# A mixer's queries, pooled input and gates as products of halves, with token-major gated branches

## The chip, the cores and the metric

The kernel runs on one core of a Trainium2 chip. The metric is the device time of one execution in microseconds. A core has five engines that run their own queues of instructions in order: TensorE (PE in the profile, with its weight loads as PEld), VectorE (DVE), ScalarE (ACT), GpSimd (POOL, which here only issues transfers) and SyncE (SP, which issues transfers). Matmuls write PSUM, and VectorE and ScalarE read it from there.

## The reference

A decoder trunk of two layers on 512 tokens of 1024 channels, all float32. Each layer is FFN, mixer, FFN; the FFN is SwiGLU with 2816 hidden channels. The mixer is what changes:

```python
h = rmsnorm(x, ln_mix[l])
z = h @ w_in[l]                       # 1024 -> 512 + 512 + 256 + 2 * 1024
u_pool, q, k, v, gate_logits = jnp.split(z, splits, axis=-1)
a = pool_mixer(u_pool, pool_w[l], pool_scale[l]) @ w_pool_branch[l]
...                                   # q, k: norm per head, rotation of 16 channels
b = swa_sink_attention(q, k, v, sinks[l]) @ w_attn_branch[l]
g_pool, g_attn = jnp.split(jax.nn.sigmoid(gate_logits), N_BRANCHES, axis=-1)
x = x + (g_pool * a + g_attn * b) @ w_out[l]
```

The pooling takes trailing means over 2, 4, 8 and 16 positions in four groups of 128 channels, less the token, then a 128x128 map per group. The attention has 8 query heads of 64 channels on 2 key heads, blocks of 128 tokens that read their own block and the one before, and a sink in the softmax.

## The kernel before

**Precision.** A float32 product is made of three matmuls of a faster float32 form: each operand is split into a high part (a cast on ScalarE, `wh` for weights) and the rest (a subtraction on VectorE, `wl`), and high x high, high x low and low x high are added in PSUM (`term`).

**Products of halves.** `strassen` forms a product whose tokens, inner channels and outer channels are each cut in halves by seven products of sums of halves where eight would be plain. The seven have the names a11, s1, s2, a12, s3, s4, a22 (`ORDER`). Each is 24 matmuls of 512 columns, 12 for each of two weight chunks; the activation is the stationary operand, the weight columns move through, and so the result has tokens on the partitions. After each a step evacuates or combines PSUM. All FFN products and w_out go that way before the change. The mixer's other products are plain: the queries and keys with moving weights, the pooled input (`u`), the gates and the branches with the weights stationary, so that channels are on the partitions (`gemm`, `tile_of`).

**Weights.** `Weights` holds a plan of chunks of 128x1024 (0.5 MB). `prep`, called after each chunk, makes the low part for two chunks ahead (3 buffers), the high part for three ahead (4 buffers), adds the sums of s2 and s4 on VectorE (`add_up`), and lets SP fetch, up to seven chunks in flight. For s1 and s3, POOL issues a second, accumulating transfer onto the chunk, which waits until the first has landed.

**The mixer** (`mix`). After the norm's operands (`Norm.feed`: x is transposed by TensorE, scaled, split), the order is two tiles of `u` begun, keys and values, the rest of `u`, queries, two more tiles of `u`, 16 gate tiles, eight steps of the two branches, then w_out by `strassen`. The row scale of the norm is spread over the partitions by two matmuls (`spread`) and multiplied in at the evacuation of each channel-major tile. Beside the tiles runs side work in generators, and tables of numbers (`HEADS`, `ATT`, `POOL`) say at which half tile each next step of a generator is written into the queues (`side`): normalising the heads, the eight attention steps (`attend`: scores, mask and maximum, exponentials, scaling, transposes of the probabilities, product with the values, split) and the four windows of the pooling. One unit of these tables is 12 matmuls. The instructions keep the order in which the program writes them, engine by engine.

All instructions go through a wrapper, so the profile has one line for them: L97. They are told apart by the names of their tiles: `wh`, `wl` weights; `raw` a loaded chunk; `sums` a sum of halves; `mm` and `sc` PSUM banks of the products; `pt`, `pt_tp`, `pt_pv` PSUM banks for transposes and side work; `xgh`, `xgl`, `more` the norm's operands; `ze`, `zo` gates and branches; `s`, `p`, `den` the attention's.

Of the kernel before, what the change touches and what calls it, by code (L numbers as in the profile page):

```python
# [10 lines left out]
F32 = mybir.dt.float32  # L11
# [17 lines left out]
PLACE = {B11: 0, T1: 1, B21: 2, B22: 3}  # L29
# [17 lines left out]
KEYS = (-3,)  # L47
NORMS = (-1, -1, 1)
HEADS = ((0, 2, 2), (0, 3, 3), (5, 8, 8), (12, 15, 15))
ATT = tuple(tuple(4 + 3 * n + d for d in (0, 1, 2, 5, 6, 9, 10)) for n in range(8))  # L50
POOL = ((-3, -2, 0, 0), (-2, -1, 8, 8), (12, 14, 17, 17), (18, 20, 25, 25))
# [4 lines left out]
C_UT = C_LT + P  # L56
C_COS = C_UT + P
# [5 lines left out]
def _consts():  # L63
# [5 lines left out]
    c[:, C_UT:C_UT + P] = i[:, None] > i[None, :]  # L69
# [50 lines left out]
def trunk(ctx, tc, x0, xT, consts, vecs, rows, w_g4, w_g3, w_d8, w_d6, w_qkv, w_u, w_pool, w_gate, w_br, w_out, out):  # L120
# [14 lines left out]
    onesr = cp.tile([P, P], F32R, name="onesr")  # L135
# [3 lines left out]
    nc.vector.tensor_copy(out=onesr, in_=ones)  # L139
# [44 lines left out]
    class Weights:  # L184
# [3 lines left out]
        def __init__(self):  # L188
# [3 lines left out]
            for l in range(L):  # L192
                for f in range(2):
                    if f == 1:
                        for kind, src, n in (("u", w_u[l], 2), ("qkv", w_qkv[l], 6), ("u", w_u[l, 2:], 2),
                                             ("gate", w_gate[l], 2 * KT), ("br", w_br[l], KT)):
                            for i in range(n):
                                self.add(kind, CH, src[i])
                        self.block(lambda h, k, c, w=w_out[l]: w[h, 2 * k + c], (CH, CH), ORDER)
# [26 lines left out]
        def block(self, w, sizes, order, start=False):  # L226

            name, first = {}, len(self.loads)
            src = {"a11": ((0, 0), None), "s1": ((1, 0), (1, 1)), "s3": ((0, 0), (1, 0)), "a12": ((0, 1), None),
                   "a22": ((1, 1), None), "s2": (None, None), "s4": (None, None)}  # L230
            for k in order:
                for c in range(2):
                    s, m = (None if p is None else w(*p, c) for p in src[k])
                    name[k, c] = self.add(k, sizes[c], s, m)
            for c in range(2):
                name["s2", c]["of"] = name["a11", c], name["s1", c]
                name["s4", c]["of"] = name["s2", c], name["a12", c]
                for k in ("a11", "s1", "a12"):
                    name[k, c]["uses"] += 1
            loads = ("a11", "s1") if start else ("s1", "a11")  # L240
            self.loads[first:] = [name[k, c] for k in (*loads, "a12", "s3", "a22") for c in range(2)]
# [48 lines left out]
        def low(self, upto):  # L290
            while len(self.lo) < min(upto, len(self.hi)):
# [7 lines left out]
                tick(2)  # L299

# [63 lines left out]
    def rsqrt(y, v):  # L364
        for step in rsqrt_steps(y, v):
            step()


    parts = [xp.tile([P, 2, NB], F32, name=f"part{i}") for i in range(2)]

    class Norm:
        def __init__(self, gain, halves):
            self.gain, self.halves = gain, halves
            self.acc = None
            self.h = self.rstd = None
# [3 lines left out]
        def opened(self):  # L379
            if self.h is None:  # L380
                self.h, self.l = (xl.tile([P, KT * S], F32R, name=n) for n in ("xgh", "xgl"))
                form, shape = ("p (i k t) -> p i k t", dict(i=4, k=4)) if self.halves else (
                    "p (q i k t) -> p q i k t", dict(q=4, i=2, k=2))
                self.h, self.l = (t.rearrange(form, **shape) for t in (self.h, self.l))
# [10 lines left out]
        def both(self, i, j):  # L395
            if i in PLACE:
                return [t[:, PLACE[i], 2 * j:2 * j + 2, :].rearrange("p k t -> p (k t)") for t in (self.h, self.l)]
# [6 lines left out]
        def feed(self, q, i, pt):  # L404
# [15 lines left out]
            if not self.halves:  # L420
                halve(*(t[:, q, i].rearrange("p k t -> p (k t)") for t in (self.h, self.l)), scaled(temp("xg")))
                return
# [6 lines left out]
            else:  # L429
                self.keep[3 - i, j] = scaled(temp("xg"))  # L430
                halve(*self.both(B22 if i else B21, j), self.keep[3 - i, j])

# [50 lines left out]
        def split_plain(self, k, b12, src):  # L483
# [5 lines left out]
            else:  # L489
                split(*(t[:, 2:4, k - 4, :] for t in (self.h, self.l)), halves(src), scale=g)  # L490
# [15 lines left out]
        def sums(self, acc=None, pt=None):  # L506
# [11 lines left out]
            if self.halves:  # L518
                self.nrstd = xp.tile([P, NB], F32, name="nrstd")
                slow.extend(rsqrt_steps(self.rstd, v))  # L520
                slow.append(lambda: nc.vector.tensor_scalar(
                    out=self.nrstd, in0=self.rstd, scalar1=-1.0, scalar2=None, op0=ALU.mult
                ))
                return
            rsqrt(self.rstd, v)
            hi, lo = sp.tile([P, NB], F32R, name="rs_h"), sp.tile([P, NB], F32, name="rs_l")
            nc.vector.tensor_copy(out=hi, in_=self.rstd)
            nc.vector.tensor_tensor(out=lo, in0=self.rstd, in1=hi.bitcast(F32), op=ALU.subtract)
            self.diag = [tp.tile([P, NB, P], F32R, name="diag", tag="t") for _ in range(2)]
            for d, r in zip(self.diag, (hi.bitcast(F32), lo)):  # L530
                nc.vector.tensor_tensor(out=d, in0=bc(ident, NB), in1=bc(r, P, 2), op=ALU.mult)

        def spread(self, pr):
            for i, d in enumerate(self.diag):
                nc.tensor.matmul(pr, onesr, d.rearrange("p b t -> p (b t)"), start=i == 0, stop=i == 1)
            self.R = xp.tile([P, S], F32, name="R")
            nc.scalar.copy(out=self.R, in_=pr)

        def terms(self, w):
            return pairs(w, [[t[:, k // 2, :, k % 2, :] for t in (self.h, self.l)] for k in range(KT)])  # L540

# [9 lines left out]
    def left(nm):  # L551
        last = [(lambda bank, q=q: nm.feed(q, 0, bank)) for q in (2, 3)]
        if nm.halves:
            step = lambda f: [(lambda bank, j=j: f(j)) for j in range(2)]
            last = step(nm.t3) + step(nm.t2) + last + step(nm.t3_split) + step(nm.t4)
        pend.extend(last)

    def feeds(nm, *banks):
# [5 lines left out]
        if nm.halves:  # L564
# [3 lines left out]
    def strassen(roles, order, n, sizes, operand, steps, mid={}):  # L568
        A, C, Dd = roles
        bank = {"a11": A, "s2": A, "s3": A, "a22": A, "s1": C, "s4": C, "a12": Dd}  # L570
        seen = set()
        for kind in order:
            pt, first = bank[kind], id(bank[kind]) not in seen
            seen.add(id(pt))
# [25 lines left out]
        order_.reverse()  # L600

    @with_exitstack
    def ffn(ctx, nm, nxt, last):
# [9 lines left out]
        def open_sums():  # L613
            W.sums = sums
            W.low(W.used + LO)
            W.add_up(W.used + HI + 1)
            W.high(W.used + HI)
            W.low(W.used + LO)
            W.load()

        wide = lambda name: ep.tile([P, 2, S], F32, name=name)
        f, ops, turns = {}, {}, []

        rs = lambda b: nm.rstd[:, b:b + 1]
        nrs = lambda b: nm.nrstd[:, b:b + 1]
        count = [0]

        def block(n, i, order, mid):
# [4 lines left out]
            def a11(pt):  # L633
                nc.scalar.copy(out=r, in_=pt)
                if W.sums is None:
                    open_sums()
                return flush
# [47 lines left out]
            turns.append((r, i, 0, n))  # L685
            turned(tile_["p"], i, 1, n)

        def high(name, src, n):

            ops[name] = op.tile([P, 2, 2, S], F32R, name="op", tag=f"op{AT[name]}")  # L690
            hi, lo = (ops[name][:, i, :, :n] for i in range(2))
            nc.scalar.copy(out=hi, in_=src)
            ops[name, "low"] = lambda: nc.vector.tensor_tensor(
                out=lo, in0=src, in1=hi.bitcast(F32), op=ALU.subtract
            )

        def low(name):
            ops.pop((name, "low"))()

        def turned(src, i, t, n):  # L700


            jn = n // P
            for q in range(2):
                for j in range(jn):
                    nc.tensor.transpose(turn[:, q, j * P:(j + 1) * P], src[:, q, j * P:(j + 1) * P], ident)
            pt = turn[:, :, :n]
            if i == 0 and t == 1:
                f["b"] = fp.tile([P, 2, S], F32, name="fb")[:, :, :n]
                nc.scalar.copy(out=f["b"], in_=pt)  # L710
            elif i == 0:
                high("a11", pt, n)
                f["a"] = fp.tile([P, 2, S], F32, name="fa")[:, :, :n]
                nc.vector.tensor_tensor(out=f["a"], in0=pt, in1=f["b"], op=ALU.subtract)
                high("s1", f["a"], n)
            elif t == 1:
                f["c"] = fp.tile([P, 2, S], F32, name="fc")[:, :, :n]
                nc.scalar.copy(out=f["c"], in_=pt)
                nc.vector.scalar_tensor_tensor(
                    out=f["a"], in0=f["a"], scalar=-1.0, in1=f["c"], op0=ALU.mult, op1=ALU.subtract  # L720
                )
                high("s2", f["a"], n)
            else:
                high("a12", pt, n)
                ops["t4"] = lambda: nc.vector.scalar_tensor_tensor(
                    out=f["a"], in0=f["a"], scalar=-1.0, in1=pt, op0=ALU.mult, op1=ALU.subtract
                )

        def flush():
            if turns:  # L730
                turned(*turns.pop(0))

        def plain(n, xt, acc, later):
# [67 lines left out]
            for h, name in ((1, "p"), (0, "r0")):  # L801
# [6 lines left out]
                turns.append((u, 0, h, n))  # L808

        def down(n, final):  # L810

# [643 lines left out]
```

## Time and profile before

| | us |
|---|---|
| median of three runs | 1845.34 (1844.85 to 1845.99) |
| profiled execution | 1845.1, its span 1843.3, granted clock 1.00 |
| TensorE busy in the span | 1835.9 |
| VectorE | 1453.9 |
| ScalarE | 1051.8 |
| POOL | 165.8 |

The first mixer lies at about 339 to 598 us of the span, the second at about 1255 to 1515; the four FFN fill the rest. The profile's views used below are the page (busy time, chain of waits, queues), the table of who waited for whom, the groups of instructions, the timeline and the table of stages. A matmul's duration on the page is its latency; matmuls overlap, and their pace is read from start to start.

### The profile page before, as it was taken

The numbers are of one execution on the slowest core, as the hardware profiler recorded it, in microseconds if no ns is written. First come the engines' busy times: TensorE is split into PE (matmuls) and PEld (weight loads), VectorE is DVE, ScalarE is ACT, GpSimd is POOL, SyncE is SP. The second block draws the span as 40 slices with busy tenths as digits, with TensorE's granted clock in tenths as the row PEclk, the third lists the DMA queues.
The fourth block names the chain that finished last, engine by engine and source line by source line (L and its number), as shares of the span: only waits on it lengthen the run. The fifth ranks groups of instructions, "written<-read, shape, count | busy, mean of one in ns | idle before, by whom it ended". The sixth has DMA issues, their size and how long they took to land.

```text
span 1843.3 us, 24049 instructions
## 1 busy us (share of the span) xinstructions
PE 1835.9 (100%) x8880; PEld 1548.6 (84%) x8880; DVE 1453.9 (79%) x1825; ACT 1051.8 (57%) x1533; POOL 165.8 (9%) x190
## 2 busy tenths in 40 slices
PE   9999999999999999999999999999999999999999
PEld 9988888887788889988888898888877888899887
DVE  8878878667669988887898878786675699878877
ACT  6655555645447664555675555565554477546554
POOL 0110101000001011110100111110000011101000
PEclk9999999999999999999999999999999999999999
DMA  8887867322247777787867778773222478777964
GB/s 257 207 232 191 220 172 195 131 81 69 81 114 193 203 176 191 187 233 185 204 162 207 169 183 233 200 189 109 92 69 82 124 171 221 179 186 183 243 183 126
DMA packets 97462, 314.85 MB, mean 171 GB/s; under 512 B 10528, under 2 KB 10784, under 8 KB 97344
## 3 DMA queue, kind: packets, MB, share of 16 engines
q1 hardware_dynamic: 67680, 225.57, 35.6%
q0 software_dynamic: 29520, 87.71, 28.2%
q8 instruction: 70, 1.15, 0.2%
q14 instruction: 48, 0.39, 0.1%
q10 hardware_dynamic: 144, 0.03, 0.0%
HBM read 295.44 MB, written 2.10 MB: 161 GB/s over the span
## 4 chain that ended last, share of the span: by engine, by line
PE 94%; DVE 3%; ACT 2%; issue 0%; DMA 0%; SPq 0%; DVEq 0%; ACTq 0%
PE mm L97 86%; PE sc L97 3%; PE pt L97 3%; PE pt_pv L97 1%; DVE wl L97 1%; ACT wh L97 1%; DVE more L97 0%; PE pt_tp L97 0%; ACT s L97 0%; DVE sums L97 0%; DVE hss L97 0%; ACT xg L97 0%; DVE win L97 0%; DMA op<-in_xT 0%; ACT p L97 0%
## 5 line engine op out<-in xcount | busy, mean ns | idle before, releaser
L97 ACT CAST wh<-raw 128x1024 fp32r<-128x1024 f32 (+3 forms) x447 | 438.8, 989 | 298.3 <-PE mm L97 160.6
L97 DVE TENSOR_TENSOR wl<-raw,wh 128x1024 fp32r<-128x1024 f32 (+3 forms) x447 | 509.7, 1146 | 93.3 <-PE mm L97 59.5
L97 PE MATMUL mm<-wh,op 128*128 128x512 f32 x1360 | 433.0, 393 | 0.0
L97 PE MATMUL mm<-wh,more 128*128 128x512 f32 (+1 forms) x1104 | 334.0, 373 | 0.0
L97 PE MATMUL mm<-wh,xgh 128*128 128x512 f32 (+2 forms) x840 | 312.1, 372 | 0.9 <-ACT xg L97 0.8
L97 PE MATMUL mm<-wh,xgl 128*128 128x512 f32 (+2 forms) x840 | 309.3, 368 | 0.0
L97 PE MATMUL mm<-wl,xgh 128*128 128x512 f32 (+2 forms) x840 | 309.2, 368 | 0.1
L97 PEld LDWEIGHTS mm<-wh,op 128*128 128x128 f32 x1360 | 255.0, 188 | 53.1 <-DVE op L97 1.4
L97 PE MATMUL mm<-wl,op 128*128 128x512 f32 x680 | 265.0, 390 | 0.0
L97 PEld LDWEIGHTS mm<-wh,more 128*128 128x128 f32 x1104 | 205.1, 188 | 29.8
L97 PE MATMUL mm<-wl,more 128*128 128x512 f32 (+1 forms) x552 | 205.8, 373 | 0.0
L97 DVE TENSOR_TENSOR wl<-sums,wh 128x1024 fp32r<-128x1024 f32 (+2 forms) x148 | 168.7, 1140 | 45.1 <-ACT wh L97 29.4
L97 ACT CAST wh<-sums 128x1024 fp32r<-128x1024 f32 (+2 forms) x148 | 144.2, 984 | 72.3 <-DVE sums L97 29.6
L97 PEld LDWEIGHTS mm<-wh,xgh 128*128 128x128 f32 x840 | 157.8, 188 | 23.2 <-ACT xg L97 2.1
L97 PEld LDWEIGHTS mm<-wh,xgl 128*128 128x128 f32 x840 | 157.8, 188 | 21.5
L97 PEld LDWEIGHTS mm<-wl,xgh 128*128 128x128 f32 x840 | 157.9, 188 | 21.2 <-DVE wl L97 0.4
L97 PEld LDWEIGHTS mm<-wl,op 128*128 128x128 f32 x680 | 127.8, 188 | 25.7 <-DVE wl L97 0.6
L97 POOL DMA_DIRECT2D raw<-in_w_g x92 | 78.7, 855 | 716.7 <-DMA raw<-in_w_g 318.2
L97 PE MATMUL mm<-xgh,wh 128*128 128x512 f32 x320 | 129.1, 404 | 0.0
L97 PE MATMUL mm<-xgl,wh 128*128 128x512 f32 x320 | 125.3, 391 | 0.0
L97 PE MATMUL mm<-xgh,wl 128*128 128x512 f32 x320 | 125.2, 391 | 0.0
L97 PEld LDWEIGHTS mm<-wl,more 128*128 128x128 f32 x552 | 103.6, 188 | 15.7 <-DVE wl L97 0.9
(264 smaller groups left out, 2332.2 us busy)
## 6 DMA issues: line engine op xcount, KB each, us to landing
raw<-in_w_g SPq DMA_DIRECT2D x160, 512.0 KB, 5.5
raw<-in_w_d SPq DMA_DIRECT2D x100, 512.0 KB, 4.5
raw<-in_w_g POOLq DMA_DIRECT2D x64, 512.0 KB, 5.9
raw<-in_w_g SPq DMA_DIRECT2D x77, 384.0 KB, 4.9
raw<-in_w_d POOLq DMA_DIRECT2D x40, 512.0 KB, 5.5
raw<-in_w_gate SPq DMA_DIRECT2D x32, 512.0 KB, 3.3
raw<-in_w_g POOLq DMA_DIRECT2D x28, 384.0 KB, 5.7
raw<-in_w_out SPq DMA_DIRECT2D x20, 512.0 KB, 3.5
```

What stands on the lines that cost most here:

```text
L97: return lambda *args, **kw: self.tc.keep_in_program_order(call(*args, **kw))
```

## The change

The queries with the pooled input, and the gates in two blocks, become products of halves by `strassen`, with weight columns moving. Keys and values are done between the first and the second of the seven products of the queries. Results are now token-major: the pooled input is turned by TensorE (`turned_u`, two groups of eight transposes per layer), the row scale is a scale per partition on ScalarE, and `spread` goes. The branches are computed with weight columns moving too, so a gated branch is token-major as an FFN's hidden state is; the class `Down`, cut out of the FFN unchanged but for its parameters, turns it (four groups of eight transposes per layer) and multiplies by w_out. The gates use two double PSUM banks (`pair`); the third serves the scores. In the blocks of queries and gates, s4's weights are no longer added by VectorE: once the low part of s2 is made, POOL issues a transfer that adds the further columns onto the same chunk (`moved`, `then`). The side work is cut into more steps, and its tables are new; the probabilities are copied by ScalarE, and one mask is spared by taking differences of neighbouring value blocks (`step_v`). The norm's operands lie in more, smaller tiles.

```diff
-ATT = tuple(tuple(4 + 3 * n + d for d in (0, 1, 2, 5, 6, 9, 10)) for n in range(8))
-POOL = ((-3, -2, 0, 0), (-2, -1, 8, 8), (12, 14, 17, 17), (18, 20, 25, 25))
+START = 3
+HEADS = ((-2, 0, 0), (1, 4, 4), (6, 10, 10), (10, 13, 13))
+ATT = tuple(tuple(START + 3 * n + d for d in (0, 1, 2, 3, 4, 5, 6, 7, 9, 10, 11)) for n in range(8))
+POOL = ((2, 3, 16, 18, 19, 20, 21), (9, 12, 20, 21, 22, 23, 24), (15, 18, 20, 23, 25, 26, 27), (20, 21, 22, 24, 26, 27, 27))
...
-                        for kind, src, n in (("u", w_u[l], 2), ("qkv", w_qkv[l], 6), ("u", w_u[l, 2:], 2),
-                                             ("gate", w_gate[l], 2 * KT), ("br", w_br[l], KT)):
...
+                        src = lambda h, k, c, w=w_uq[l]: w[h, 2 * k + c]
+                        self.block(src, (CH, CH), ORDER, True, [("kv", w_kv[l, c]) for c in range(2)], True)
+                        for i in range(2):
+                            self.block(lambda h, k, c, w=w_gate[l, i]: w[h, 2 * k + c], (CH, CH), ORDER, moved=True)
...
+                if moved:
+                    name["s2", c]["then"] = name["s4", c], w(0, 1, c)
+                else:
+                    name["s4", c]["of"] = name["s2", c], name["a12", c]
...
+                if "then" in c:
+                    after, part = c["then"]
+                    after["raw"] = c["raw"]
+                    nc.gpsimd.dma_start(out=c["raw"][:, :n], in_=part, accum_op=ALU.add)
...
-        def spread(self, pr):
-            for i, d in enumerate(self.diag):
-                nc.tensor.matmul(pr, onesr, d.rearrange("p b t -> p (b t)"), start=i == 0, stop=i == 1)
...
-        A, C, Dd = roles
+        A, C, Dd = roles if len(roles) > 2 else (*roles, roles[1])
...
+            yield
+            for j in range(G):
+                nc.scalar.activation(out=s[:, j, :], in_=s[:, j, :], func=AF.Copy, scale=den[:, j:j + 1])
...
+            nc.scalar.copy(out=p0, in_=pt)
...
-        for i in range(2 * KT):
-            tile_of(
-                "gate", 2 + i, lambda pt: nc.vector.tensor_tensor(out=z[i], in0=pt, in1=nm.R, op=ALU.mult)
-            )
...
+        def turned_u(src, half):
+            for q in range(2):
+                pt = side_bank[q]
+                for g in range(4):
+                    nc.tensor.transpose(pt[:, g * P:(g + 1) * P], src[:, q, g * P:(g + 1) * P], ident)
+                at = half * HT + q * P
+                nc.scalar.copy(out=us[:, :, at:at + P], in_=pt.rearrange("p (g t) -> p g t", g=4))
...
+        def branch(i, t, pt, acts, w, between):
+            for c in range(2):
+                for q in range(2):
+                    for k in range(2):
...
+        left_over = queries()
+        pair = roles[:2]
+        z = []
+        for i in range(2):
+            z.append(gates(i, pair, left_over if i == 0 else None))
...
+                branch(i, t, pt, [(out["ah"][:, k, :], out["al"][:, k, :]) for k in range(4)], w, between)
+                y, v = z[i]["ru"[t]], z[i]["dp"[t]]
+                if (i, t) == (0, 0):
+                    dn.turned(z[0]["u"], 0, 1, S)
+                nc.vector.tensor_tensor(out=v, in0=pt, in1=v, op=ALU.mult)
+                add(y, y, v)
```

How the change moves instructions, at three places. First VectorE's queue beside the gates, at the pooling's window of 16 (`win`); `zo` is a gate being evacuated before, `zr` and `zu` are gates now, `us` and `more` the pooled input's operands. Before:

```order
L97 TENSOR_TENSOR win<-win 128x504
L97 TENSOR_TENSOR zo_2992<-mm_2984,R 128x512
L97 TENSOR_TENSOR wl<-raw,wh 128x1024
L97 TENSOR_TENSOR p_4026<-pt_tp,cst 128x512
L97 TENSOR_TENSOR p_4028<-pt_tp,cst 128x512
L97 TENSOR_TENSOR al<-pt_pv,ah 128x2x128
L97 COPY_PREDICATED s<-cst,sc 128x512
```

And of the change:

```order
L93 TENSOR_TENSOR win<-win 128x504
L93 TENSOR_TENSOR wl<-raw,wh 128x1024
L93 TENSOR_TENSOR den<-den,es 128x4
L93 RECIPROCAL den<-den 128x4
L93 TENSOR_TENSOR more<-us,more 128x512
L93 TENSOR_TENSOR dl<-us,dh 128x512
L93 TENSOR_TENSOR win<-win,cst 128x16
L93 SCALAR_TENSOR_TENSOR us<-win,us 128x512
L93 TENSOR_TENSOR zr<-zr,mm_2988 128x1024
L93 TENSOR_TENSOR wl<-sums,wh 128x1024
L93 TENSOR_TENSOR p_4310<-p_4229,cst 128x512
L93 COPY_PREDICATED s<-cst,mm_2986 128x512
```

A low half of a weight chunk (`wl`) now stands before and after a gate's evacuation, which is 1024 columns wide where it was 512.

Second, TensorE's queue in the attention's branch, a place that has no counterpart before; `zu` is a gated branch, `ah` and `al` the attention's result:

```order
L93 MATMUL mm_4686<-wh,ah 128x512
L93 MATMUL mm_4686<-wl,ah 128x512
L93 MATMUL mm_4686<-wh,al 128x512
L93 MATMUL pt<-cst,zu 128x128 x8
L93 MATMUL mm_4684<-wh,ah 128x512
```

A group of eight transposes of the gated branch stands between two products.

Third, POOL's queue from the end of one FFN (`in_w_d`) to the next (`in_w_g`). Before:

```order
L97 DMA x<-u 128x2x512
L97 MEMSET s 128x512 x2
L97 DMA raw<-in_w_out 128x1024 x4
L97 DMA x<-zo_2993 128x2x512 x3
L97 DMA raw<-in_w_g 128x1024 x8
```

And of the change:

```order
L93 DMA x<-u 128x2x512
L93 DMA raw<-in_w_uq 128x1024 x4
L93 DMA raw<-in_w_gate 128x1024
L93 DMA sums<-in_w_uq 128x1024 x2
L93 DMA raw<-in_w_gate 128x1024 x4
L93 DMA sums<-in_w_gate 128x1024 x2
L93 DMA raw<-in_w_gate 128x1024 x3
L93 DMA sums<-in_w_gate 128x1024 x2
L93 DMA raw<-in_w_out 128x1024 x4
L93 DMA x<-aside 128x2x512 x2
```

Eighteen accumulating loads of weights per layer now stand where there were none, six of them onto sums (`sums<-`).

More of the change, by code (lines that the diff above doesn't have):

```diff
@@ L55 @@
 C_LT = C_LQ + P
-C_UT = C_LT + P
-C_COS = C_UT + P
+C_COS = C_LT + P
 C_SIN = C_COS + NB * ROT
@@ L224, in add, with block @@
             return c
-        def block(self, w, sizes, order, start=False):
+        def block(self, w, sizes, order, start=False, between=(), moved=False):
             name, first = {}, len(self.loads)
@@ L362, in rsqrt_steps, with __init__ @@
         ]
-    def rsqrt(y, v):
-        for step in rsqrt_steps(y, v):
-            step()
     parts = [xp.tile([P, 2, NB], F32, name=f"part{i}") for i in range(2)]
     class Norm:
-        def __init__(self, gain, halves):
-            self.gain, self.halves = gain, halves
+        def __init__(self, gain, mixer=False):
+            self.gain, self.mixer = gain, mixer
             self.acc = None
-            self.h = self.rstd = None
+            self.one = self.rstd = None
             self.part = parts[0]
@@ L379, in opened @@
         def opened(self):
[L380 to L384, printed above, removed]
+            if self.one is None:
+                self.one = {i: [xl.tile([P, 4, HT], F32R, name="xg", tag=f"{t}{side}") for side in range(2)]
+                            for i, t in ((B11, "b11"), (T1, "t1"))}
+                self.two = [xl.tile([P, 2, 4, HT], F32R, name="xg2", tag=f"b2{side}") for side in range(2)]
                 self.more, self.keep = {}, {}
@@ L489, in split_plain @@
             else:
-                split(*(t[:, 2:4, k - 4, :] for t in (self.h, self.l)), halves(src), scale=g)
+                split(*(t[:, :, k - 4, :] for t in self.two), halves(src), scale=g)
         def square(self, k, src, acc):
@@ L552, in left @@
         last = [(lambda bank, q=q: nm.feed(q, 0, bank)) for q in (2, 3)]
[L553 to L556, printed above, removed]
+        step = lambda f: [(lambda bank, j=j: f(j)) for j in range(2)]
+        if nm.mixer:
+            pend.extend([lambda bank, j=j: [nm.b12(j), nm.t3(j)] for j in range(2)] + last + step(nm.t1) + step(nm.t2))
+        else:
+            pend.extend(step(nm.t3) + step(nm.t2) + last)
+        pend.extend(step(nm.t3_split) + step(nm.t4))
     def feeds(nm, *banks):
@@ L563, in feeds @@
         }
-        if nm.halves:
+        if not nm.mixer:
             mid["a22", 1, 1] = lambda: [nm.t1(j) for j in range(2)]
@@ L684, in block @@
             )
[L685 to L694, printed above, removed]
-            )
[L697 to L731, printed above, removed]
+            dn.turns.append((r, i, 0, n))
+            dn.turned(tile_["p"], i, 1, n)
         def plain(n, xt, acc, later):
@@ L892, in ffn @@
+                dn.turns.append((u, 0, h, n))
         xt = acc = None
@@ new lines, in mix, with between @@
+        spare = up.tile([P, 4, S], F32, name="aside", tag="us")
+        dn = Down(
+            turn, op_of, lambda name: z_tile("f" + name, dict(b="p", a="d", c="u")[name]),
+            lambda i: spare[:, 2 * i:2 * i + 2, :], 1.0, nxt,
+        )
+        for i in range(2):
+            w = [W.take("br") for _ in range(2)]
+            for t in (1, 0):
+                pt = roles[2 if t else 1]
+                def between(i=i, t=t):
+                    if i and t:
+                        dn.turned(z[0]["r"], 0, 0, S)
+                        dn.low("a11")
+                    if not t:
+                        W.prep()
+                branch(i, t, pt, [(out["ah"][:, k, :], out["al"][:, k, :]) for k in range(4)], w, between)
[4 more added lines that the diff above has]
+                add(y, y, v)
+                if not t:
+                    W.prep()
@@ L1337, in trunk @@
+        dn.turns.append((z[1]["r"], 1, 0, S))
+        dn.down(S, True, roles, {("a11", 0, 0): lambda: dn.low("s1"), ("a11", 0, 1): lambda: dn.turned(z[1]["u"], 1, 1, S)})
     gain = lambda l, i: vec[:, l, i * KT:(i + 1) * KT]
-    nm = first = Norm(gain(0, 0), True)
+    nm = first = Norm(gain(0, 0))
     def begin(xt):
```

766 lines of the change are left out of this document (400 added, 366 removed).

## The prediction

> **What bounds the kernel now.** The page comes first: the busy shares and the chain of waits. Then, for TensorE alone, the list of who waited for whom, because a matmul's end is modelled and a busy share of 100% proves little.
>
> ```profile
> span 1843.3 us, 24049 instructions
> PE 1835.9 (100%) x8880; PEld 1548.6 (84%) x8880; DVE 1453.9 (79%) x1825; ACT 1051.8 (57%) x1533; POOL 165.8 (9%) x190
> PE 94%; DVE 3%; ACT 2%; issue 0%; DMA 0%; SPq 0%; DVEq 0%; ACTq 0%
> ...
> PE cold L97 <- DVE warm_in L97: 1.1, 1, 1.1
> PE mm L97 <- ACT xg L97: 0.8, 3, 0.3
> PE pt_pv L97 <- ACT qkv L97: 0.5, 2, 0.3
> PE pt_tp L97 <- DVE zo L97: 0.5, 2, 0.2
> ```
>
> The last four rows are all that TensorE waited for in 1843 us: 2.9 us, of which 1.1 is the start. So the time is the number of matmuls times their pace, and what does not change the queue of TensorE, or make it wait, is worth nothing. The pace is read from the chain in order of time (start, us, what), in a stretch of FFN where nothing else is on TensorE, and around one group of eight transposes:
>
> ```profile
> 850.13 32.69 PE mm L97 x144
> 883.70 5.49 PE mm L97 x24
> 890.06 22.31 PE mm L97 x100
> ```
>
> 144 matmuls of 512 columns take 32.69 us: 0.227 us each. The 24 that start at 883.70 end at 889.19, and the next piece begins at 890.06: between them lies one group of eight 128x128 transposes, 0.87 us with the change-over on both sides.
>
> The stages (start:end, length, then busy us and count of PE, PEld, DVE, ACT, POOL, granted clock, DMA share, GB/s) show how full the helpers are while TensorE does not wait:
>
> ```profile
> 396.00:508.00 112.00, 111.76 (x558) 85.48 (x556) 74.79 (x168) 54.37 (x144) 0.00 (x0) 1.00 0.23 77
> 555.00:600.00 45.00, 45.00 (x212) 37.22 (x211) 40.66 (x43) 35.06 (x57) 7.01 (x7) 1.00 0.78 195
> 613.00:930.00 317.00, 316.75 (x1530) 272.91 (x1531) 263.83 (x273) 190.09 (x242) 36.46 (x41) 1.00 0.76 194
> ```
>
> The first is the attention with most gates of layer 0: VectorE at 67%, ScalarE at 49%, DMA at 0.23. The second is the w_out product (VectorE 90%, ScalarE 78%), the third a whole FFN (VectorE 83%, DMA 0.76). Both dense stages run without a wait of TensorE worth a row above. So the mixer's front has room, and I know how full the helpers may be.
>
> **What the change removes on TensorE.** Per layer, the queries (4 chunks x 24 = 96 matmuls of 512 columns), the pooled input (96) and the gates (16 x 24 = 384) are 576 plain matmuls. As products of halves each goes from eight to seven: 3 blocks x 7 x 24 = 504. That is 72 fewer. The two matmuls that spread the row scale (`spread`) go too: 74 per layer, 148 in both, x 0.227 = 33.6 us. Keys and values keep 96 of 256 columns, the branches 192, w_out 168; attention and pooling keep theirs.
>
> [...] The chain's 227 ns at a granted clock of 1.00 is what this kernel pays, and the sum keeps it.
>
> **What it adds there.** Token-major results have to be turned: the pooled input in two groups of eight transposes, the gated branches in four. Six groups per layer, twelve in all, x 0.87 = 10.4 us. They are on the path: nothing hides work on TensorE.
>
> **VectorE and ScalarE.** Their prices are paces, from start to next start where the engine was not waiting:
>
> ```profile
> 602.86 2.35 DVE L97 TENSOR_TENSOR sums<-raw 128x1024 f32<-128x1024 f32 x2
> 605.13 0.68 DVE L97 TENSOR_TENSOR more<-more 128x512 fp32r<-128x512 f32 x1
> 605.73 1.22 DVE L97 TENSOR_TENSOR wl<-sums,wh 128x1024 fp32r<-128x1024 f32 x1
> ...
> 456.65 1.03 ACT L97 CAST wh<-raw 128x1024 fp32r<-128x1024 f32 x1
> 457.58 0.58 ACT L97 COPY s<-sc 128x512 f32<-128x512 f32 x1
> 458.06 0.36 ACT L97 CAST ah<-pt_pv 128x256 fp32r<-128x256 f32 x1
> ```
>
> VectorE: 1.135 us for 1024 columns (2.27 for two), 0.60 for 512. ScalarE: 0.93 and 0.48. A weight chunk now feeds 12 matmuls (2.72 us) where it fed 24, so per layer 18 more chunks are split. With the sums of halves and wider evacuations, and fewer 512-wide ones, I count over both layers on VectorE 118 more of 1024 columns, 22 fewer of the strided 1024-column ones, 72 fewer of 512: 134 - 25 - 43 = +66 us; on ScalarE about +80 us by the same count. None of it is on the path as long as it fits, and the tightest place is the two gate blocks with the attention: 28 chunks. VectorE has there 28 low halves, 4 sums and 8 evacuations of 1024 (40 x 1.135 = 45.4), 41 of 512 (24.6), and 95 small ones for which I take 0.15 to 0.3 us, 16: 86 us. TensorE needs 28 x 2.72 = 76 us for the products and, for seven attention steps, what such a step adds to 36 matmuls now:
>
> ```profile
> 455.14 1.13 PE L97 MATMUL sc<-qkv 64*128 64x256 f32 x8
> 466.08 1.14 PE L97 MATMUL sc<-qkv 64*128 64x256 f32 x8
> ```
>
> 10.94 us from one to the next, less 36 x 0.227 = 8.17: 2.77 each, 19 in all; with turns, heads and windows (4) 100 us. So VectorE is at 86%: between the FFN (83%) and w_out (90%), which both run dense. ScalarE, by the same count 74 us, is at 74%. In the table of instructions the order holds: a late helper is caught by low halves made two chunks (5.4 us) ahead and high halves three (8.2 us); the longest run in which VectorE's rows exceed TensorE's is 3 us (the window of 16 beside an evacuation), and 5 us where the branches' products and sums meet the first chunks of w_out, whose low halves have those 5.4 us.
>
> **The waits that are added.** The step of the attention that copies the scaled probabilities (ScalarE) now stands one half product (2.72 us) ahead of their transposes, where it stood three. Behind a late copy TensorE waits, and with it all that follows. The gates use two double banks in turn, so an evacuation has one product (5.4 us) until its bank is written again; it takes 1.22. No row has these waits, so bounds: below, -1.0 (the two waits on qkv and zo in the first fence vanish); above, 16 (first rival). I take +1.8, as much again as the waits of the first fence without the start, since the stages that are as full cost no more.
>
> **Loads.** 36 more accumulating transfers are issued by POOL, 12 of which add w's second column half onto a chunk that is already summed (`then` in `low`). By the queue table:
>
> ```profile
> q1 hardware_dynamic: 67680, 225.57, 35.6%
> q0 software_dynamic: 29520, 87.71, 28.2%
> ```
>
> a chunk of 0.524 MB costs the 16 engines 1.53 us plain and 3.1 us accumulating (share x span x MB). A gate block has ten plain and six accumulating: 34 us in about 50, 0.68, under the FFN's 0.76. Hidden, so zero; on SP 12 more issues stand among loads that run seven chunks ahead.
>
> **Sum.** 1845.1 (the profiled execution; span 1843.3 and 1.8 around it; median of the runs 1845.34) - 33.6 + 10.4 + 1.8 = 1823.7 us.
>
> **Rivals.** *Lateness in the gate blocks.* VectorE cannot use all its time there: it sits idle for inputs, as now:
>
> ```profile
> L97 DVE TENSOR_TENSOR ze<-mm,R 128x512 f32<-128x512 f32 x10 | 6.8, 683 | 11.9 <-PE mm L97 11.9
> L97 DVE SCALAR_TENSOR_TENSOR more<-mm,vec,more 128x512 fp32r<-128x512 f32 x4 | 3.0, 750 | 5.6 <-ACT more L97 5.6
> L97 DVE TENSOR_TENSOR den<-den,es 128x4 f32<-128x4 f32 x8 | 1.3, 157 | 4.4 <-ACT es L97 4.4
> ```
>
> (of 396 to 508). If these 22 us of forced idleness stay, 86 + 22 = 108 us exceed TensorE's 100 by 8 per layer: 1821.9 + 16 = 1838. For it: ScalarE and VectorE call each other in every half product. Against it: idleness for TensorE's own results (11.9) shrinks when VectorE is behind, and w_out at 90% has none. *The moved columns come late (slower).* The low half of s2 must be made, then POOL issues the accumulating load, and ScalarE's cast of s4 waits for it, and TensorE for that; s4's cast comes five chunks, 13.6 us, after. The rows:
>
> ```profile
> L97 POOL DMA_DIRECT2D raw<-in_w_out x8: 844/853/882, 510.3 to 1473.2; - x8
> ...
> raw<-in_w_g POOLq DMA_DIRECT2D x15, 512.0 KB, 5.7
> ```
>
> 0.85 to issue, 5.7 to land: 6.6 us, so 7 to spare, unless POOL, which takes its issues in turn and stops at each for a plain load to land, is three or four behind. There are 12 such loads; from an average of 1.9 us beyond the slack the 23.2 us are gone, and at 4 us the time is 1821.9 + 48 = 1870.
>
> [...]
>
> *The turns cost nothing*, because the group's price holds change-overs that the removed parts had too: up to 1845.1 - 33.6 = 1811.5. Against it: groups of transposes in the middle of products are what the 0.87 was read from. *The change does not do what it says*: the order of the changed kernel has 148 fewer matmuls of 512 columns and 96 more of 128, so only a lower pace could take the gain back.
>
> **How the numbers follow.** Forecast 0.75 (1823.7, own range 1819 to 1831), lateness 0.14 (1838, 1832 to 1846), late columns 0.07 (1870), turns free 0.04 (1811.5). The range 1817 to 1837 holds the first and half of the second. About 0.2%, 3.7 us, is what a measurement of this kernel tells from none. Faster by more: the first, the last and most of the second, 0.88; within: 0.05; slower: the third, 0.07.
>
> **What will show it.** Right: 8880 - 52 = 8828 matmuls or so (records can be missing), the waits of TensorE still under 5 us, the gate blocks about 100 us long with VectorE near 86% and ScalarE near 75%. Wrong: a row of TensorE waiting for `s` or `wh` of ScalarE or `wl` of VectorE with several us (first rival), ScalarE's `wh` or POOL waiting for a transfer of the gate weights with TensorE behind it (second), groups of transposes that take less than 0.8 us (third), or a pace above 0.23 us per matmul in the gate blocks.

## The result, and the profile after

The changed kernel takes 1823.12 us, median of four runs (1822.47 to 1827.11), the kernel before 1845.12 beside it: a ratio of 0.9884, interval 0.9867 to 0.9902, 22.0 us. The forecast was 1823.7. The profiled execution is the longest of the four, 1827.11 with a span of 1825.1; the other three lie within 0.8 us of each other. These 4 us have a place in the trace, and it is one that the prediction did not name. In one experiment below (14 additions per layer) one of the four executions took 3888.18 us; its median is that of the other three.

First the page of the changed kernel: span and busy time by engine.

```profile
span 1825.1 us, 24191 instructions
PE 1815.0 (99%) x8828; PEld 1531.7 (84%) x8828; DVE 1512.7 (83%) x1828; ACT 1133.7 (62%) x1635; POOL 192.5 (11%) x220
```

8828 matmuls, as announced. VectorE has 58.8 us more, ScalarE 81.9 (66 and 80 were said). Then who waited for whom on TensorE (us in total, times, longest):

```profile
PE pt_pv L93 <- DVE al L93: 3.2, 1, 3.2
PE cold L93 <- DVE warm_in L93: 1.1, 1, 1.1
PE mm L93 <- ACT xg L93: 0.8, 3, 0.3
PE mm L93 <- DVE wl L93: 0.2, 1, 0.2
```

TensorE waits for 5.3 us in all, and 3.2 of them are one wait.

The table of stages of the changed kernel. The 336 matmuls of layer 0's two gate blocks run from 391.4 to 491.4 us, and the branches' products begin at 492.6. The rows are the gate blocks, a piece early in them, their end, the start of the branches, and the w_out product:

```profile
391.40:491.40 100.00, 99.80 (x501) 77.06 (x499) 94.44 (x182) 82.01 (x182) 8.52 (x10) 1.00 0.63 165
409.00:446.00 37.00, 37.00 (x186) 28.53 (x186) 36.05 (x67) 28.42 (x69) 3.28 (x4) 1.00 0.69 182
456.00:491.40 35.40, 35.40 (x180) 26.80 (x177) 33.62 (x62) 31.07 (x76) 0.00 (x0) 1.00 0.38 116
491.40:503.00 11.60, 11.60 (x60) 8.46 (x59) 5.21 (x6) 9.06 (x15) 1.70 (x2) 1.00 0.85 189
545.00:590.00 45.00, 45.00 (x215) 37.33 (x214) 41.83 (x43) 34.48 (x56) 5.81 (x6) 1.00 0.71 171
```

The gate stage is 100 us long, as counted, and fuller than counted: VectorE is busy for 94.4 of the 100 us (86 was said), ScalarE for 82 (74 was said). VectorE is at 97% in the early piece and still at 95% in the late one; behind the gates, in the branches, it is at 45%. TensorE does not wait in either piece. One expectation below speaks of 76% from 475 to 503 us: that stretch reaches past the end of the gates, where VectorE has less to do.

The one long wait lies in layer 1. The timelines of SP, ScalarE, VectorE and TensorE there (start, us, what, and in brackets the idle time before it and what ended it):

```profile
1350.03 0.43 SPq L93 DMA_DIRECT2D praw<-in_w_pool  x1
...
1361.28 0.62 ACT L93 CAST w_pool<-praw 128x512 fp32r<-128x512 f32 x1 [4.92 <-DMA praw<-in_w_pool]
...
1361.93 0.69 DVE L93 TENSOR_TENSOR w_pool<-praw,w_pool 128x512 fp32r<-128x512 f32 x1 [4.96 <-ACT w_pool L93]
1362.54 0.41 DVE L93 TENSOR_TENSOR al<-pt_pv,ah 128x256 fp32r<-128x256 f32 x1
...
1363.01 0.65 PE L93 MATMUL pt_pv<-p,qkv 128*64 128x256 f32 x4 [3.20 <-DVE al L93]
```

The pooling's 128x128 maps (`w_pool`) are fetched two half products before they are split. Here the load landed 11.2 us after its issue. ScalarE, VectorE and TensorE stand behind one another: the row of TensorE names VectorE, but VectorE had waited for ScalarE, and ScalarE for a transfer.

Then the granted clock (the column after POOL's) in two stretches behind the wait:

```profile
1364.00:1367.00 3.00, 3.00 (x12) 2.02 (x11) 2.90 (x8) 3.00 (x5) 0.00 (x0) 0.51 0.51 173
1368.00:1370.00 2.00, 2.00 (x11) 1.64 (x10) 1.73 (x6) 1.19 (x5) 0.00 (x0) 1.00 0.81 262
```

From 1364 us on, 1 us after the wait's end, TensorE runs at half its clock for 3.4 us. By the starts of its matmuls the 3.2 us of waiting cost 4.8: the last one before the wait (1359.43) and one behind the slow stretch (1370.44) are 11.0 us apart, and the same two 6.2 us apart in the run with the earlier load below.

### The profile page after: what moved, and what is told of

The parts are those of the page before. It is cut to its first block, busy times and chain, and to the rows that moved or that the text cites. A ratio compares the mean times of both kernels' runs of the same rounds, so it can differ in the third digit from the quotient of the medians.

```text
span 1825.1 us, 24191 instructions
## 1 busy us (share of the span) xinstructions
PE 1815.0 (99%) x8828; PEld 1531.7 (84%) x8828; DVE 1512.7 (83%) x1828; ACT 1133.7 (62%) x1635; POOL 192.5 (11%) x220
## 4 chain that ended last, share of the span: by engine, by line
PE 95%; DVE 3%; ACT 1%; DMA 1%; issue 0%; DVEq 0%; ACTq 0%; SPq 0%
PE mm L93 89%; PE pt L93 3%; DVE wl L93 1%; PE pt_pv L93 1%; PE pt_tp L93 1%; DMA praw<-in_w_pool 1%; DVE more L93 0%; DVE sums L93 0%; ACT wh L93 0%; ACT xg L93 0%; PE cold L93 0%; ACT p L93 0%; DVE xg L93 0%; DVE win L93 0%; DVE m L93 0%
## 5 line engine op out<-in xcount | busy, mean ns | idle before, releaser
L93 PE MATMUL mm<-wh,xg 128*128 128x512 f32 (+2 forms) x2032 | 613.7, 373 | 0.9 <-ACT xg L93 0.8
L93 PE MATMUL mm<-wh,more 128*128 128x512 f32 (+1 forms) x1520 | 472.9, 380 | 0.0
L93 PEld LDWEIGHTS mm<-wh,xg 128*128 128x128 f32 x2032 | 375.4, 188 | 59.0 <-ACT xg L93 2.1
L93 PE MATMUL mm<-wl,xg 128*128 128x512 f32 (+2 forms) x1016 | 376.2, 370 | 0.2 <-DVE wl L93 0.2
L93 PEld LDWEIGHTS mm<-wh,more 128*128 128x128 f32 x1520 | 283.5, 188 | 51.3 <-issue 4.6
L93 PE MATMUL mm<-wl,more 128*128 128x512 f32 (+1 forms) x760 | 287.5, 378 | 0.1
L93 PEld LDWEIGHTS mm<-wl,xg 128*128 128x128 f32 x1016 | 191.1, 188 | 27.3 <-DVE wl L93 1.0
L93 DVE SCALAR_TENSOR_TENSOR x<-mm,x 128x1024 f32<-128x1024 f32 (+1 forms) x84 | 86.2, 1040 | 13.2 <-PE mm L93 13.0
L93 DVE TENSOR_TENSOR sums<-raw 128x1024 f32<-128x1024 f32 (+1 forms) x86 | 95.4, 1148 | 0.0
L93 DVE TENSOR_TENSOR sums<-sums,raw 128x1024 f32<-128x1024 f32 (+1 forms) x74 | 84.2, 1138 | 0.0
```

What stands on the lines that cost most here:

```text
L93: return lambda *args, **kw: self.tc.keep_in_program_order(call(*args, **kw))
```

## The experiments

All kernels below are the changed kernel with one edit. A figure with a sign is the median less that of the kernel before on the same chip, set against the change's own -22.0: +10 means ten us slower than the change. Medians of the kernel before in the three sets were 1845.86, 1845.95 and 1846.38, so differences of about 1 us say nothing.

**The matmuls put back.** In the products of the queries and the gates the matmul that opens a product is issued several times (`again` is 3 or 4 there):

```diff
-    nc.tensor.matmul(pt[:, q, :n], s, m[:, k, :], start=first and c == k == j == 0, ...)
+    opens = first and c == k == j == 0
+    for _ in range(1 + opens * again.get(kind, 0)):
+        nc.tensor.matmul(pt[:, q, :n], s, m[:, k, :], start=opens, ...)
```

> In the products of halves of the queries and the gates the matmul that opens an accumulation is issued four times (five for a11 and s1 of the gates); it overwrites, so the result is the same. 74 matmuls of 512 columns per layer, 148 in both, as many as the change removed. Theory A (the time is the number of matmuls by their pace): +148 x 0.227 = +33.6 us, 1857 (1854 to 1858, since helpers get more room and 1 to 3 us of waits may go). Theory B (the saved matmuls were partly paid back by helpers that are late in the gate blocks, and the time is set by them there): less than +28 us, below 1851, because the added matmuls fill waits.

1855.94, +32.1 us with 8976 matmuls: 0.217 us each, and 1.5 us less than 148 x 0.227. Theory A: the change's gain is the matmuls it takes away. Where the 1.5 us are is not shown: the added matmuls run at the pace of the others (five of them from 361.31 to 362.45 us, 0.228 each), TensorE's rows of waits are no shorter (2.4 us, against 2.1 in the changed kernel without its long wait), and two medians are not told apart much better than this.

**The turns twice.** `in_mixer[0]` is true while a mixer is being written.

```diff
-                for q in range(2):
+                for q in (0, 1, 0, 1) if in_mixer[0] else (0, 1):
                     for j in range(jn):
                         nc.tensor.transpose(turn[:, q, j * P:(j + 1) * P], src[:, q, j * P:(j + 1) * P], ident)
...
-                for g in range(4):
+                for g in (0, 1, 2, 3, 0, 1, 2, 3):
                     nc.tensor.transpose(pt[:, g * P:(g + 1) * P], src[:, q, g * P:(g + 1) * P], ident)
```

> Each of the twelve groups of eight transposes that the change added is done twice in the same place, 96 transposes more; the result is the same. Theory A (the turns are paid in full on TensorE): four transposes take 0.35 us from start to next start in the trace after, so 96 cost 8.4 us: 1831.5 (1830 to 1833). Theory B (the turns are free, in the shade of a change-over or of waits for the helpers): under +3 us.

1834.11, +10.3 us: more than both theories said, and what was too low is my figure of 0.35 us for four. The timelines of TensorE around the same group of transposes show it, first in the changed kernel:

```profile
528.24 0.39 PE L93 MATMUL mm<-wh,al 128*128 128x512 f32 x1
528.47 1.03 PE L93 MATMUL pt<-cst,zu 128*128 128x128 f32 x8
529.26 0.48 PE L93 MATMUL mm<-wh,ah 128*128 128x512 f32 x1
529.58 0.40 PE L93 MATMUL mm<-wl,ah 128*128 128x512 f32 x1
```

and with the turns doubled:

```profile
530.28 1.91 PE L93 MATMUL pt<-cst,zu 128*128 128x128 f32 x16
531.95 0.48 PE L93 MATMUL mm<-wh,ah 128*128 128x512 f32 x1
532.26 0.40 PE L93 MATMUL mm<-wl,ah 128*128 128x512 f32 x1
```

From the start of the transposes to the start of the next matmul it is 0.79 us for eight and 1.67 for sixteen: a further eight cost 0.88. And the first matmul behind a group takes 0.31 to 0.32 until the next starts where others take 0.23, so eight alone cost 0.79 + 0.09 = 0.88 too. My 0.35 had left out that tail. Twelve groups more are 10.6 us by this, and 10.3 were measured: the turns are paid whole.

**The sums back on VectorE.**

```diff
-    self.block(src, (CH, CH), ORDER, True, [("kv", w_kv[l, c]) for c in range(2)], True)
+    self.block(src, (CH, CH), ORDER, True, [("kv", w_kv[l, c]) for c in range(2)])
...
-        self.block(lambda h, k, c, w=w_gate[l, i]: w[h, 2 * k + c], (CH, CH), ORDER, moved=True)
+        self.block(lambda h, k, c, w=w_gate[l, i]: w[h, 2 * k + c], (CH, CH), ORDER)
```

> The moved column halves are undone: in the blocks of queries and gates s4's weights are again the sum of s2's and a12's chunk, made by VectorE, and POOL issues 12 accumulating loads fewer. VectorE has 12 additions of 1024 columns more, 13.6 us in both layers, nearly 11 of them in the gate blocks. Theory A (both ways are hidden): the median within 1.5 us of 1823. Theory B (VectorE has no room left in the gate blocks, forced idleness counted): +5 to +13 us. Theory C (the accumulating loads hold up the loads beside them, w_pool's among them): 1 to 4 us faster.

1828.24, +4.4 us: not hidden. Theory B said +5 to +13, so the size is just below it, and C has the wrong sign. TensorE's waits:

```profile
PE pt_pv L93 <- DVE al L93: 3.0, 5, 0.9
...
PE mm L93 <- DVE wl L93: 1.0, 3, 0.5
```

Five waits for `al`, the low part of the attention's result, in both gate stages. The moved column halves, which the prediction priced at zero, are worth these 4.4 us: with VectorE at 94% in the gate blocks there is little cover left.

**More work on VectorE, in four doses and places.** One edit each, in the function that issues the side work of a half product `t`:

```diff
+        spin = xp.tile([P, S], F32, name="spin")
         def side(t):
+            for _ in range(t % 2 if 0 <= t < 28 else 0):   # 14 per layer; the others: 1 (28), 4 <= t < 14, 18 <= t < 28
+                nc.vector.tensor_tensor(out=spin, in0=cst[:, 0:S], in1=cst[:, 0:S], op=ALU.add)
```

> In every other half product of the two gate blocks VectorE makes one addition of 512 columns more on a tile that nothing reads: 14 per layer, 14 x 0.60 = 8.4 us in each gate stage, 16.8 in both. Theory A (by the prediction: VectorE has 14 us of room per layer and all of it can be used): under +2 us, 1825 at most. Theory B (by the trace after VectorE is at 95% from 398 to 436 us and 91% to 475, and much of what is left is forced idleness): a third to a half of the added work comes out on TensorE, as 13.6 us of sums cost 5 us: +6 to +8 us, 1829 to 1831, as waits of TensorE for al and wl.

> The same in every half product: 28 per layer, 16.8 us in each gate stage, 33.6 in both. Theory A (14 us of room per layer): 2.8 us too much per layer, +6 us, 1829. Theory B (the room is used up at the first dose): what the second 16.8 us add comes out whole, +17 to +25 us in all, 1840 to 1848: no faster than the kernel before.

> Ten additions of 512 columns per layer on VectorE that nothing reads, one in each of the half products 4 to 13 of the gate blocks, ahead of the place where TensorE waited for al in the two runs with 14 and 28: 6.0 us per layer, 12.0 in both. Theory A (VectorE's share over the whole gate stage decides): as the 16.8 us of the run with 14 gave +11, these give about +8 us, 1831, and so do ten late ones. Theory B (a backlog decides that has grown by about 445 us, and what lies in front of it counts): +6 to +10 us, with the wait for al near 445 and 1354 us, but late ones are free.

> The same ten additions per layer in the half products 18 to 27, where VectorE is at 76% in the trace after (475 to 503 us); 12.0 us in both layers. Theory A (the share over the whole stage): about +8 us, 1831. Theory B (the backlog near 445 us): under +2 us, 1825 at most, and no wait for al above 0.5 us.

| additions per layer | added on VectorE, both layers | median | measured |
|---|---|---|---|
| 14, every other half product | 16.8 us | 1834.19 (1831.31 to 1837.35) | +10.2 |
| 28, every half product | 33.6 | 1844.50 | +20.6 |
| 10, half products 4 to 13 | 12.0 | 1837.63 | +13.3 |
| 10, half products 18 to 27 | 12.0 | 1827.13 | +2.8 |

With 28 the whole gain is gone, as theory B said: the ratio to the kernel before is 0.9993, interval 0.9984 to 1.0003. The prediction's 14 us of room per layer do not exist: 8.4 us per layer already cost more than half their length, somewhat more than the +6 to +8 of theory B. The last two rows tell place from amount. The same ten additions cost more than their own length when they come early and a quarter of it when they come late, so the share of the stage does not decide (theory A is out), nor does the share in pieces, 97% against 95%. Theory B has the early ones costlier than the late ones, but both sizes were too low: +6 to +10 and under +2 were said, and the late ones do make TensorE wait. The waits of TensorE, ten early:

```profile
PE pt_pv L93 <- DVE al L93: 6.7, 2, 3.4
PE mm L93 <- DVE wl L93: 2.7, 4, 0.9
```

and the timeline of VectorE in it, up to the end of one of the two long waits (`spin` is the added work):

```profile
445.41 0.69 DVE L93 TENSOR_TENSOR spin<-cst 128x512 f32<-128x512 f32 x1
446.01 0.69 DVE L93 TENSOR_TENSOR p<-p,cst 128x512 f32<-128x512 f32 x1
...
448.56 1.22 DVE L93 TENSOR_TENSOR wl<-raw,wh 128x1024 fp32r<-128x1024 f32 x1
449.70 0.42 DVE L93 TENSOR_TENSOR al<-pt_pv,ah 128x256 fp32r<-128x256 f32 x1
```

VectorE goes from one row to the next without a gap: it has fallen behind in the stretch where it is at 97%, and the small result that TensorE needs at once, `al`, comes that much late. No single instruction is slow there: `wl` takes 1.22 us and `al` 0.42, in the changed kernel 1.22 and 0.41. The sizes fit: all ten additions, 6.0 us, stand ahead of this `al`, VectorE had 1.0 us idle there in the changed kernel (409 to 446), and TensorE waits 4.7 us in layer 0. With ten late ones the waits for `al` are 3.8 us in three. In layer 0 six additions, 3.6 us, stand ahead of the one that TensorE waits for, at 480.67; VectorE had 1.5 us idle from 456 to 480, and the wait is 1.6 us. The other four stand behind it, and no `al` after them is waited for: VectorE has the room of the branches there.

**The probabilities' copy late.**

```diff
-ATT = tuple(tuple(START + 3 * n + d for d in (0, 1, 2, 3, 4, 5, 6, 7, 9, 10, 11)) for n in range(8))
+ATT = tuple(tuple(START + 3 * n + d for d in (0, 1, 2, 3, 5, 5, 6, 7, 9, 10, 11)) for n in range(8))
```

> The attention's scaled copies on ScalarE are written into the queues in the half product of their transposes, ahead of them, in place of one half product earlier; nothing else is moved. In the trace after, a step's four copies end 1.3 us before the transposes. Theory A (a wait behind ScalarE falls on TensorE, step by step): the copies stand behind a high half (1.05 us) and themselves take 1.28, so each of the 16 steps makes TensorE wait 1 to 2 us for s: +16 to +32 us, 1839 to 1855. Theory B (ScalarE, at 74 to 80%, has caught up by then and the place in its queue is of no weight): under +4 us.

1833.27, +9.3 us: 0.58 us for each of the 16 steps, between the two theories. The row of TensorE's waits for the copies:

```profile
PE pt_tp L93 <- ACT s L93: 4.5, 6, 1.3
```

The timeline of one step, TensorE and then ScalarE:

```profile
421.16 0.39 PE L93 MATMUL mm<-wh,more 128*128 128x512 f32 x1
422.43 1.21 PE L93 MATMUL pt_tp<-cst,s 128*128 128x128 f32 x4 [0.88 <-ACT s L93]
423.40 0.48 PE L93 MATMUL mm<-wh,more 128*128 128x512 f32 x1
...
421.03 1.05 ACT L93 CAST wh<-sums 128x1024 fp32r<-128x1024 f32 x1 [2.72 <-DVE s L93]
421.98 1.28 ACT L93 ACTIVATE s<-s,den 128x128 f32<-128x128 f32 x4
```

TensorE waits 0.88 us for the first of four copies, and then, without a row for it, for each of the others: four transposes take 0.97 us until the next matmul, where they take 0.36 in the kernel of the change. Not every step costs that: from the matmul before to the matmul behind, three of the 16 steps take no longer than in the change, and the longest takes 2.1 us more. So 1 to 2 us each was too much. The place of an instruction in ScalarE's queue is a cost on TensorE, and one half product ahead is just enough.

**The moved columns late.** `held` starts empty; `lo` counts the low parts made, `i` is the chunk's place among them.

```diff
-                    nc.gpsimd.dma_start(out=c["raw"][:, :n], in_=part, accum_op=ALU.add)
+                    self.held.append((i + 4, c["raw"][:, :n], part))
+            while self.held and len(self.lo) > self.held[0][0]:
+                _, to, part = self.held.pop(0)
+                nc.gpsimd.dma_start(out=to, in_=part, accum_op=ALU.add)
```

> POOL's twelve accumulating loads that make s4's weights out of s2's are written into its queue four chunks (10.9 us) later, one chunk (2.7 us) ahead of ScalarE's cast of the result; issue and landing take 6.6 us, so the cast is about 4 us late. Theory A (the prediction's price for late columns: each is paid by its lateness): 12 x 3.9 = +47 us, 1870. Theory B (the high half is needed three chunks, 8.2 us, after the cast; ScalarE's queue stands still for 4 us at the first chunk of each block and less at the second, and what is behind it are evacuations with one product of room): +0 to +15 us, 1823 to 1838, as waits of TensorE for s or mm behind ScalarE.

1855.54, +31.6 us, slower than the kernel before: between the theories again, about midway. The waits of TensorE and of ScalarE:

```profile
PE pt_tp L93 <- ACT s L93: 13.8, 2, 8.4
PE mm L93 <- ACT wh L93: 6.8, 2, 3.5
PE mm L93 <- DVE wl L93: 3.4, 5, 1.3
...
ACT wh L93 <- DMA sums<-in_w_gate: 23.4, 3, 12.2
ACT wh L93 <- DMA sums<-in_w_uq: 20.6, 4, 10.3
```

and ScalarE's timeline at the first late chunk of layer 0's gates:

```profile
435.82 1.04 ACT L93 CAST wh<-sums 128x1024 fp32r<-128x1024 f32 x1 [12.19 <-DMA sums<-in_w_gate]
436.77 0.40 ACT L93 ACTIVATE s<-s,den 128x128 f32<-128x128 f32 x1
```

ScalarE stands still for 12.2 us, not 4, because the transfer needs longer than the 6.6 us I had worked with: in this run the gates' columns land after 8.3 us and the queries' after 11.8, in the median. What TensorE misses first is not the weight but the copies that stand behind the cast in ScalarE's queue. Only two places per layer stop TensorE, with 24 us of waits in all; much of the other 7.6 us is the clock, by an estimate: 3 us at 0.50 cost 1.5 us here, which makes 6 us if all four places have them. The stages at that wait and behind it:

```profile
428.00:437.00 9.00, 0.81 (x4) 0.35 (x2) 2.65 (x7) 1.18 (x2) 0.00 (x0) 0.81 0.95 229
437.00:440.00 3.00, 2.78 (x8) 2.15 (x9) 1.73 (x2) 2.74 (x8) 0.00 (x0) 0.50 0.03 5
```

**The pooling's weights earlier, and later.**

```diff
-            praw = temp("praw")
+            praw = sp.tile([P, S], F32, name="praw")
...
-        for g, at in zip(work, [(1, 2), (15, 17), *HEADS, *ATT, *POOL]):
+        for g, at in zip(work, [(1, 2), (7, 17), *HEADS, *ATT, *POOL]):
```

The later one has (17, 17) there, and the buffer of the change.

> The load of w_pool is issued eight half products earlier (unit 7 in place of 15, into a buffer of its own), its split stays at unit 17. Theory A (the load stands too late on SP; where it lands late, VectorE waits for its split and TensorE, for al, behind VectorE): the row of TensorE waiting 3.2 us for al and VectorE's 4.96 us before w_pool go, the profiled execution falls from 1827.1 by 3 to 4.5 us to about 1823, and the median by 0 to 3 us, to 1820 to 1823. Theory B (the wait is made by VectorE's own queue at this place, the window of 16 and the evacuations, and the load only came last): a wait of 2 us or more of TensorE for al or another tile of VectorE stays near 1360 us of the span, and the time stays at 1823 to 1827.

> The load of w_pool is issued in half product 17 in place of 15, right ahead of its split; the split stays. Theory A (its landing, 7.8 and 11.2 us after the issue in the trace after, is what VectorE and, behind it, TensorE wait for): VectorE waits 8 to 11 us in each layer, TensorE some 1.8 us less as in the trace after (4.96 and 3.20), 6 to 9 us, and 1 to 2 us more by the lower clock behind each wait: +14 to +22 us, 1837 to 1845. Theory B (the long landing was chance, and ordinary landings are hidden even so, as the earlier issue moved the median by nothing): under +4 us.

Earlier: 1823.00 (1821.80 to 1824.41), -0.9. The wait for `al` is gone, the profiled execution is 1823.37 and TensorE waits 2.6 us in all; the median is the same. This fits theory A and not B, but it proves little alone: in no other trace of this section does TensorE wait for more than 1.3 us behind that load, though most left it in its place. It landed after 4.5 to 8.5 us in them.

Later: 1823.71, -0.7, no wait for `al` either. SP ran ahead of the half products, so the later place put the issue off by only 2 to 3 us, and the landings were quick, 6.0 and 6.2 us. An issue right ahead of the split, which theory A was about, did not come about; the time is as theory B said.

So what the 3.2 us wait hung on stands in the trace of the change, a landing of 11.2 us, and the medians say that it does not weigh on ordinary executions. The early version issues the load some 25 us sooner but is no faster than the change, and nothing here beats the change by more than can be measured. Why that one landing took 11.2 us is open.

## Why the prediction was right

**The matmuls, -33.6: right.** 148 fewer, 0.217 us each when put back, against 0.227; the 1.5 us between them are at the edge of what the medians tell.

**The turns, +10.4: right.** 0.88 us per group in the changed kernel, 0.85 in the doubled one, 0.87 in the prediction. "The turns cost nothing" is out.

**The added waits, +1.8: not told from nothing.** -33.6 + 10.6 leaves 1.0 of the measured -22.0, no more than the medians can tell, and that it is near 1.8 may be chance. Without the one long wait, TensorE's rows add up to less than before (2.1 and 2.9 us), so no added wait shows. The profiled execution had 3.2 us of waiting and a slow clock behind it, from the load of `w_pool`, which was nowhere in the prediction.

**VectorE and ScalarE "hidden as long as it fits": right result, wrong reason.** The totals were close (58.8 for 66, 81.9 for 80), the stage was not: 94.4 us on VectorE where 86 were counted. The small instructions were priced about right (88 of them, 17 us busy, for 95 and 16); the counts that failed are those of 512 columns, 50 where 41 were counted, and of the low halves, 30 for 28. The room per layer was 5.6 us, not 14. And 86% "between the FFN (83%) and w_out (90%)" is no measure of room: w_out runs dense at 93%, while in the gate stage six more us per layer, early, cost 6.6. What differs is that the attention asks VectorE for small results at once. The rival "lateness in the gate blocks" was the right mechanism at a dose that the change stays just short of: 8.4 us more per layer bring the time to 1834, near its 1838.

**The moved columns, "hidden, so zero": two sizes were wrong and one term was left out.** They land later than 6.6 us after the issue begins (the row's 5.7 us already count from the start of the issue, so its 0.85 had gone in twice). The transfers of the changed kernel (KB each, median us to landing):

```profile
sums<-in_w_gate POOLq DMA_DIRECT2D x8, 512.0 KB, 8.0
sums<-in_w_uq POOLq DMA_DIRECT2D x4, 512.0 KB, 11.2
```

And ScalarE's cast can come sooner than 13.6 us after the issue, as in the first gate block of layer 0 (a row of POOL's timeline, one of ScalarE's, and the landing of this transfer alone):

```profile
406.33 1.15 POOL L93 DMA_DIRECT2D sums<-in_w_gate  x1
...
415.30 1.05 ACT L93 CAST wh<-sums 128x1024 fp32r<-128x1024 f32 x1
...
sums<-in_w_gate POOLq DMA_DIRECT2D x1, 512.0 KB, 8.9
```

Issue to cast is 9.0 us there, and the transfer needed 8.9. So the 7 us to spare were gone in this block, and in the queries ScalarE already waits, three times, with TensorE still covered by the high halves made ahead:

```profile
ACT wh L93 <- DMA sums<-in_w_uq: 5.4, 3, 2.7
```

The rival's price of one us per us of lateness was not far off: 31.6 us for delays that stopped ScalarE for 44.0 us. The term left out is the gain: without the moved columns the change would be 4.4 us slower.

**The issues on POOL** took the 0.85 us that the prediction had, except behind one another. Those of the gates' moved columns, ns least, median and most in the changed kernel, with VectorE at 94%:

```profile
L93 POOL DMA_DIRECT2D sums<-in_w_gate x8: 844/856/1147, 406.3 to 1357.3; - x8
```

Six of the eight take 0.84 to 0.86 us. The two of 1.15 us, and the four of the queries (1.19 to 1.51), began while the issue before them on POOL was still running. What was late was late by the transfer.

## What to carry to other kernels

Where one engine does all the work on the path, its instruction count by its pace gives the gain within 1 or 2 us in 1800, and a group's price must include the longer start of what follows it. Before a helper's work is called hidden, look for the results that the bound engine wants at once, and count the helper's idle time ahead of each: 6.0 us of added work ahead of such a result, where VectorE had 1.0 us idle, made TensorE wait 4.7 us, and the share over the stage did not tell this place from one where the same work cost a quarter. A wait of some 3 us on TensorE can bring the half clock behind it and is to be priced with it: 4.8 us for 3.2 here.

## What the hardware showed that was not expected

The half clock can follow waits of about 3 us, and not by their length alone. With 14 additions per layer TensorE waited 2.71 us in layer 0 (up to 448 us) and 2.71 in layer 1 (up to 1357). The stretches behind the two waits:

```profile
449.00:451.00 2.00, 2.00 (x10) 1.19 (x8) 1.93 (x6) 1.20 (x2) 0.00 (x0) 0.50 0.90 188
1358.00:1360.00 2.00, 2.00 (x14) 1.36 (x12) 1.97 (x6) 2.00 (x4) 0.86 (x1) 1.00 0.82 264
```

Half clock behind the first, full clock behind the second. So the length of a wait does not decide alone, and what else does is not shown. With ten early additions the waits for `al` are 3.3 us in layer 0 and 3.36 in layer 1. Behind the second the eight matmuls `mm<-qkv` take 2.08 us, as in the slow stretch of the changed kernel, against 1.14 in the next step; around the first the granted clock is 1.00 (436 to 475 us). The half clock also spreads executions: the ten early additions gave 1834.22 us at a mean granted clock of 0.999 and 1837.46 to 1837.94 at 0.997 to 0.998.
